# Where the low halves of streamed weights are made: by a GpSimd subtraction, or by an accumulating DMA

## The chip, the cores and the metric

The program runs on one core of a Trainium2 chip. The metric is the device time of one execution in microseconds. The kernel before takes 3158.84 us (median of three runs, 3158.76 to 3171.22).

Engines go by short names here: PE multiplies matrices (PEld loads its weights), DVE, ACT and POOL (GpSimd) do elementwise work, SP issues DMAs. Each engine works through its own list in order, and semaphores hold it where it needs another's result. Sixteen DMA engines move data between HBM and the on-chip SBUF for whoever issues a transfer.

## The reference

One decoder layer for a prompt of 2048 tokens and a sample batch of 8 x 8 tokens, width 1024. Cut to what carries work here:

```python
def hybrid_layer(x, c, r0, s0_re, s0_im, pos0, w_ada, b_ada, norm1_g, norm2_g, w_in, ...):
    mod = (jnp.einsum('bd,de->be', jax.nn.silu(c), w_ada) + b_ada).astype(x.dtype)
    sh1, sc1, gt1, sh2, sc2, gt2 = jnp.split(mod[:, None, :], 6, axis=-1)
    h = rms_norm(x, norm1_g) * (1 + sc1) + sh1
    z = jnp.einsum('bld,de->ble', h, w_in)
    q, k, v, g, u, gate_r, gate_s = jnp.split(z, IN_SPLITS, axis=-1)
    ...
    ret, r_new = retention(q, k, v.reshape(...), r0)
    ret = rms_normalize(ret).reshape(bsz, seq_len, RET_V_W) * jax.nn.silu(g)
    ssm, s_re, s_im = s5(u, s0_re, s0_im, ...)
    ssm = jax.nn.gelu(ssm)
    ssm = ssm * jax.nn.sigmoid(jnp.einsum('blc,ce->ble', ssm, w_glu))
    branch_r = jnp.einsum('blc,cd->bld', ret, w_br)
    branch_s = jnp.einsum('blc,cd->bld', ssm, w_bs)
    merged = jax.nn.sigmoid(gate_r) * branch_r + jax.nn.sigmoid(gate_s) * branch_s
    x = x + gt1 * jnp.einsum('bld,de->ble', merged, w_out)
    h2 = rms_norm(x, norm2_g) * (1 + sc2) + sh2
    ff = jnp.einsum('blf,fd->bld', jnp.square(jax.nn.relu(jnp.einsum('bld,df->blf', h2, w_up))), w_down)
    return x + gt2 * ff, r_new, s_re, s_im
```

Everything is float32. The kernel gets its precision from a rounded format that PE takes (float32r): a number x is split into a high half hi = round(x) and a low half lo = x - hi, and a product is made of three matmuls, hi·hi, hi·lo and lo·hi.

## The kernel before, in words

**Stages.** The prompt is worked through in four super-blocks of 512 tokens; then one feed-forward stage does w_up and w_down for all tokens, with a block scheme of its own that does not pass through the lines changed here. Each super-block runs the matmul blocks u, q, k, v, g, gr0, gs0, gr1, gs1 (columns of w_in), glu, br0, br1, bs0, bs1 and wo0, wo1. Beside the second super-block's prompt rows run the sample's. The first super-block has eight blocks "ada" (columns of w_ada) between its own. In the third, w_up for the sample runs as a "side" stream (us0 to us7), in the fourth w_down (ds0, ds1): after each weight unit of the main list, one unit of the side list is used.

**The weight stream.** All these weights come through one stream of 312 units of 128 x 2 x 512 float32, 512 KB each: 86 for the first super-block, 54 for the second, 86 each for the third and the fourth. `plan` fixes the order. `fetch` (L181) loads a unit from HBM into one of four raw buffers by a DMA that SP issues. `refill` (L183 on) splits it: ACT copies the raw unit to the rounded high half `whi` (L191), and one engine subtracts, `wlo` = raw - `whi` (L194): DVE for the ada units and for half of the side units, POOL for all the others. `whi` and `wlo` have five buffers each (RING). A main unit is used by 24 prompt matmuls of 128 x 512 (L253), an ada or a side unit by 4 (L259, L227). `refills` in `block` takes up a new unit after the first quarter of the next one; in the wo blocks of the first three super-blocks (order "j") four units are held until the block's last quarter.

**Order.** The kernel is written as one program; a scheduler in the framework then sets the order of the instructions on each engine, by its own model of how long things take. So an edit of a few lines can change the order in other places. Only the first five units of the stream (`keep`) stay in the order they are written in.

**What else DVE, POOL and ACT do in these stages.** DVE: norms (L606, L610: steps of a reciprocal square root on 128 x 1 values), S5 scans (L1200), evacuation of PSUM banks. POOL: `hl` at the start (L665), part of the rotary (L1531), `sl` and `ml`, low halves of activations (L1621, L1674). ACT: copies and tanh out of PSUM.

Of the kernel before, what the change touches and what calls it, by code (L numbers as in the profile page):

```python
# [13 lines left out]
AF = mybir.ActivationFunctionType  # L14
ALU = mybir.AluOpType
# [12 lines left out]
SIDE = ('us', 'ds')  # L28
# [54 lines left out]
class Layer:  # L83
# [101 lines left out]
    def refill(self, keep=False):  # L185
        nc = self.nc
        if self.split < len(self.stream):
            raw = self.rawq.pop(self.split)
            hi = self.ring.tile([P, 2, 512], F32R, name="whi")
            lo = self.ring.tile([P, 2, 512], F32R, name="wlo")  # L190
            a = nc.scalar.activation(hi, raw, AF.Copy)  # L191
            name = self.stream[self.split][0][:2]
            eng = nc.vector if name == "ad" or name in SIDE and self.split % 4 < 2 else nc.gpsimd
            l = eng.tensor_sub(lo, raw, hi)  # L194
            if keep:
                self.tc.keep_in_program_order(a)
                self.tc.keep_in_program_order(l)
            self.wq[self.split] = (hi, lo)
            self.split += 1
        self.fetch()  # L200
# [1605 lines left out]
```

## Time and profile before

| | |
|---|---|
| Median of three runs | 3158.84 us |
| The profiled execution, device time | 3166.64 us |
| Its span in the profile | 3164.8 us |
| Mean granted PE clock | 0.958 |
| Busy: PE, DVE, POOL, ACT | 2930.6, 1942.0, 1761.4, 1219.9 us |
| Moved by DMA | 516.23 MB on SP's queue, 52.1% of the 16 engines' span |

The stages lie so in the profile (by the first matmuls of their banks): setup 0 to 63 us, the four super-blocks 63 to 523, 523 to 980, 980 to 1402 and 1402 to 1814 us, feed-forward from 1814 us on. "Idle before" and "waits" are put down to what came last; L12 is line 12 of the kernel. [...] In the change, lines after L193 stand three lines lower (L253 before is L256 after).

### The profile page before, as it was taken

How to read it: one execution, taken by the hardware profiler on the slowest of the kernel's cores; microseconds unless marked ns; L12 is line 12 of the kernel's file. 1: busy time of each engine (PE TensorE's matmuls, PEld its weight loads, DVE VectorE, ACT ScalarE, POOL GpSimd, SP SyncE). 2: the span in 40 equal slices, each digit the busy share in tenths (PEclk: the TensorE clock that was granted, in tenths of full speed). 3: DMA queues.
4: the chain of work that ended last, by engine and by line, in shares of the span. 5: the costliest groups of instructions: out<-in, count | busy, mean ns of one | idle time of the engine just before them, and what ended most of it. 6: DMA issues, size and time to landing. Idle time of an engine off the chain costs nothing. (4 is left out here: it accounts for less than half of the span.)

```text
span 3164.8 us, 37143 instructions
## 1 busy us (share of the span) xinstructions
PE 2930.6 (93%) x13436; PEld 2389.0 (75%) x13436; DVE 1942.0 (61%) x3116; ACT 1219.9 (39%) x1876; POOL 1761.4 (56%) x1028
## 2 busy tenths in 40 slices
PE   7789999999989899999899799999999999997995
PEld 3568777788777688777788687787778888876884
DVE  4979674771667875667743556655556655456554
ACT  2233442122423234423234354455334555553332
POOL 2331454334344545555345486668888666588881
PEclk9889999999999899999999899999999999998998
DMA  8466435543345954458544645556444654466442
GB/s 219 154 193 215 148 103 166 158 137 107 91 108 185 254 173 126 127 173 239 164 134 132 192 156 173 180 180 207 163 146 161 205 173 154 153 226 212 141 146 80
DMA packets 336556, 518.61 MB, mean 164 GB/s; under 512 B 71270, under 2 KB 168054, under 8 KB 332267
## 3 DMA queue, kind: packets, MB, share of 16 engines
q1 hardware_dynamic: 336372, 516.23, 52.1%
q8 instruction: 106, 1.74, 0.2%
q14 instruction: 78, 0.64, 0.1%
HBM read 401.39 MB, written 114.78 MB: 163 GB/s over the span
## 5 line engine op out<-in xcount | busy, mean ns | idle before, releaser
L194 POOL TENSOR_TENSOR wlo<-wraw,whi 128x1024 fp32r<-128x1024 f32 x248 | 613.0, 2483 | 760.8 <-ACT whi L191 655.2
L399 PE MATMUL pq_down<-shi,tw 128*128 128x512 f32 x1792 | 569.4, 397 | 36.5 <-DVE acc L459 26.1
L191 ACT ACTIVATE whi<-wraw 128x1024 fp32r<-128x1024 f32 x312 | 324.0, 1056 | 652.3 <-issue 79.6
L399 PE MATMUL pq_up<-shi,tw 128*128 128x512 f32 x1792 | 560.5, 393 | 13.2 <-ACT tw L310 7.7
L399 PEld LDWEIGHTS pq_down<-shi,tw 128*128 128x128 f32 x1792 | 342.4, 191 | 115.8 <-issue 22.5
L399 PEld LDWEIGHTS pq_up<-shi,tw 128*128 128x128 f32 x1792 | 340.2, 190 | 86.4 <-ACT tw L310 8.8
L311 POOL TENSOR_TENSOR tw<-traw,tw 128x512 fp32r<-128x512 f32 x192 | 286.9, 1509 | 146.9 <-ACT tw L310 146.5
L391 DVE TENSOR_TENSOR slo<-sw,shi 128x1024 fp32r<-128x1024 f32 x140 | 233.4, 1679 | 197.2 <-ACT shi L390 164.2
L399 PE MATMUL pq_down<-slo,tw 128*128 128x512 f32 x896 | 354.1, 395 | 0.0
L399 PE MATMUL pq_up<-slo,tw 128*128 128x512 f32 x896 | 352.2, 393 | 0.8 <-DVE slo L391 0.8
L390 ACT ACTIVATE shi<-sw 128x1024 fp32r<-128x1024 f32 x140 | 147.1, 1057 | 256.1 <-DMA sw<-sd 184.5
L459 DVE SCALAR_TENSOR_TENSOR acc<-pq_down,modT,acc 128x512 f32<-128x512 f32 x224 | 159.3, 743 | 91.7 <-PE pq_down L399 91.2
L399 PEld LDWEIGHTS pq_down<-slo,tw 128*128 128x128 f32 x896 | 171.4, 191 | 35.2
L399 PEld LDWEIGHTS pq_up<-slo,tw 128*128 128x128 f32 x896 | 170.3, 190 | 36.4 <-DVE slo L391 1.1
L310 ACT ACTIVATE tw<-traw 128x512 fp32r<-128x512 f32 x224 | 136.1, 624 | 60.9 <-PE pq_down L399 51.6
L409 ACT ACTIVATE aq<-pq_up 128x512 f32<-128x512 f32 x128 | 72.4, 590 | 183.8 <-PE pq_up L399 183.8
L194 DVE TENSOR_TENSOR wlo<-wraw,whi 128x1024 fp32r<-128x1024 f32 x64 | 85.7, 1340 | 67.9 <-ACT whi L191 63.8
L345 POOL TENSOR_TENSOR ts<-traw,ts 128x512 f32<-128x512 f32 x64 | 97.2, 1518 | 51.7 <-issue 48.8
L311 POOL TENSOR_TENSOR tw<-t,tw 128x512 fp32r<-128x512 f32 x64 | 102.4, 1611 | 33.4 <-ACT tw L310 33.4
L253 PE MATMUL pd_wo<-whi,mh 128*128 128x512 f32 x256 | 102.0, 402 | 16.2 <-DVE tw L1692 16.0
L310 ACT ACTIVATE tw<-ts 128x512 fp32r<-128x512 f32 x128 | 80.2, 626 | 91.0 <-PE pq_up L399 78.6
L345 POOL TENSOR_TENSOR ts<-traw 128x512 f32<-128x512 f32 x64 | 85.6, 1338 | 51.9 <-DMA traw<-in_w_up_dram 29.6
(531 smaller groups left out, 6726.2 us busy)
## 6 DMA issues: line engine op xcount, KB each, us to landing
wraw<-in_w_in_dram SPq DMA_DIRECT2D x144, 512.0 KB
sw<-sd SPq DMA_DIRECT2D x112, 512.0 KB
s5p<-s5c SPq DMA_DIRECT2D x32, 1024.0 KB
traw<-in_w_up_dram SPq DMA_DIRECT2D x64, 512.0 KB
sd<-sq SPq DMA_DIRECT2D x32, 1024.0 KB
sd<-aq SPq DMA_DIRECT2D x32, 768.0 KB
traw<-in_w_down_dram SPq DMA_DIRECT2D x24, 1024.0 KB
wraw<-in_w_ada_dram SPq DMA_DIRECT2D x32, 512.0 KB
```

Source lines behind the costliest of these rows:

```text
L191: a = nc.scalar.activation(hi, raw, AF.Copy)
L194: l = eng.tensor_sub(lo, raw, hi)
L253: nc.tensor.matmul(banks[j], a, b, start=(k == 0 and z == 0), stop=(k == nk - 1 and z == 2))
L310: self.nc.scalar.activation(t[:, 0], x, AF.Copy)
L311: eng.tensor_sub(t[:, 1], x, t[:, 0])
L345: G.tensor_sub(x[p], l, x[m] if isinstance(m, int) else m)
L390: nc.scalar.activation(hi[:, a], t, AF.Copy)
L391: V.tensor_sub(lo[:, a], t, hi[:, a])
L399: self.nc.tensor.matmul(bank, w, x, start=(first and a == 0 and z == 0), stop=(a == 3 and z == 2), skip_group_check=True)
L409: copy = lambda d, b: nc.scalar.activation(d, b, AF.Copy)
L459: V.scalar_tensor_tensor(d, b, g, d, op0=ALU.mult, op1=ALU.add)
```

## The change

Three things are edited in `refill`. Which engine subtracts is no longer chosen by a list: the first five units (`keep`) and the ada units are subtracted by DVE. For every other unit ACT writes the negated high half into `wlo` (a copy with scale -1 from `whi`, L196), and then a DMA that POOL issues (L197) reads the unit's weights from HBM a second time and adds them onto `wlo`: lo = -hi + raw. The rest of the program is as it was.

```diff
             a = nc.scalar.activation(hi, raw, AF.Copy)
             name = self.stream[self.split][0][:2]
-            eng = nc.vector if name == "ad" or name in SIDE and self.split % 4 < 2 else nc.gpsimd
-            l = eng.tensor_sub(lo, raw, hi)
+            if keep or name == "ad":
+                l = nc.vector.tensor_sub(lo, raw, hi)
+            else:
+                nc.scalar.activation(lo, hi, AF.Copy, scale=-1.0)
+                nc.gpsimd.dma_start(lo, self.stream[self.split][1], accum_op=ALU.add)
             if keep:
                 self.tc.keep_in_program_order(a)
                 self.tc.keep_in_program_order(l)
```

In the built program POOL's 248 subtractions are gone and 276 accumulating DMAs stand on POOL; ACT has 276 more instructions (2017 in place of 1741), DVE 28 fewer tensor operations (36 subtractions of weights in place of 64). SP issues the same 1121 DMAs. The scheduler has also moved rows on every engine. Three places:

POOL, where the third super-block begins (`ml`: low halves for its neighbour wo1; `nq`, `ab`: quarters of the normed rows, L704 and L709). Before:

```order
L1674 TENSOR_TENSOR ml<-tb,mh 128x512
L194 TENSOR_TENSOR wlo<-wraw,whi 128x1024 x9
L704 TENSOR_TENSOR nq<-ab,nq 128x512
L709 TENSOR_TENSOR ab<-ab,nq 128x512
L194 TENSOR_TENSOR wlo<-wraw,whi 128x1024 x4
```

With the change:

```order
L1677 TENSOR_TENSOR ml<-tb,mh 128x512 x4
L197 DMA wlo<-in_w_out_dram 128x2x512 x4
L197 DMA wlo<-in_w_in_dram 128x2x512
L197 DMA wlo<-in_w_up_dram 128x2x512
L197 DMA wlo<-in_w_in_dram 128x2x512
L197 DMA wlo<-in_w_up_dram 128x2x512
```

The subtractions have become DMAs, and units of the main list (`w_in`) and of the side list (`w_up`), which POOL and DVE shared before, now all stand on POOL, in turn.

ACT, a little later in the third super-block, behind the copy of a sample bank `ps_us` and the evacuation `aS`. Before:

```order
L729 ACTIVATE aS<-pas 128x4x64
L191 ACTIVATE whi<-wraw 128x1024 x7
L740 ACTIVATE st<-ps_us_7815 64x512
L191 ACTIVATE whi<-wraw 128x1024
L729 ACTIVATE aS<-pas 128x4x64
```

With the change:

```order
L732 ACTIVATE aS<-pas 128x4x64
L191 ACTIVATE whi<-wraw 128x1024
L196 ACTIVATE wlo<-whi 128x1024
L191 ACTIVATE whi<-wraw 128x1024
L196 ACTIVATE wlo<-whi 128x1024
L191 ACTIVATE whi<-wraw 128x1024
```

Each high half is now followed by the negated copy, so a run of seven splits is fourteen instructions long.

PE, first super-block, where gs0 (bank `pd_gs`) begins behind an ada block; `po`, `prt` and `pkv` are retention's. Before:

```order
L253 MATMUL pd_gs_2577<-hh,whi 128x512
L1305 MATMUL po<-vU,rw 128x128
L253 MATMUL pd_gs_2577<-hl,whi 128x512
L253 MATMUL pd_gs_2574<-hh,wlo 128x512
L253 MATMUL pd_gs_2574<-hh,whi 128x512
```

With the change:

```order
L256 MATMUL pd_gs_2601<-hh,whi 128x512
L1308 MATMUL po<-vU,rw 128x128
L256 MATMUL pd_gs_2601<-hl,whi 128x512
L1310 MATMUL po<-R,qU 128x128
L1308 MATMUL po<-vU,rw 128x128
L1310 MATMUL po<-R,qU 128x128
L1308 MATMUL po<-vU,rw 128x128
L1310 MATMUL po<-R,qU 128x128
L1308 MATMUL po<-vU,rw 128x128
L1310 MATMUL po<-R,qU 128x128
L1328 MATMUL prt<-cpk,rw 128x128 x4
L1316 MATMUL pkv<-vU,rw 128x128 x4
```

In the change the first product with `wlo` comes only behind these rows of retention: the scheduler has put work between the matmuls that need only the high half and those that need the low one.

## The prediction

> **What bounds the kernel now.** I read the page's first part, then busy time by stage, then PE's waits, then the rows of the operations that the edit touches. In the first rows of windows the columns are start and end of the stretch, its length, busy time of PE, PEld, DVE, ACT, POOL, the PE clock, the busy share of the DMA engines, and GB/s.
>
> ```profile
> span 3164.8 us, 37143 instructions
> 63.00:523.00 460.00, 413.91 (x1977) 332.81 (x1978) 356.84 (x727) 159.74 (x231) 175.86 (x83) 0.93 0.53 161
> 523.00:980.00 457.00, 436.00 (x2114) 361.47 (x2113) 254.69 (x544) 126.39 (x197) 182.65 (x95) 0.96 0.43 125
> 980.00:1402.00 422.00, 391.73 (x1882) 325.42 (x1881) 291.37 (x509) 154.27 (x225) 223.65 (x104) 0.96 0.59 173
> 1402.00:1814.00 412.00, 380.94 (x1812) 318.31 (x1812) 242.67 (x413) 146.19 (x196) 201.24 (x93) 0.96 0.57 173
> ```
>
> The four super-blocks, 1751 us, are the only stage in which the weight stream runs. PE sets their length: it idles 46 + 21 + 30 + 31 = 128 us there. POOL, whose work is taken away, is busy for about 45% of them, and is no bound. Who ends PE's idle time? PE's waits, longest first (total, times, longest):
>
> ```profile
> PE pd_wo L253 <- DVE tw L1692: 16.0, 3, 10.0
> PE py L1215 <- DVE s5t L1207: 14.6, 8, 3.5
> PE pd_k L253 <- DVE rt L1530: 12.5, 3, 10.2
> PE pt L650 <- DVE xr L643: 9.4, 4, 2.7
> PE pms L735 <- DVE mS L1655: 8.9, 1, 8.9
> PE pw L1128 <- DVE s5bx L1121: 8.0, 1, 8.0
> PE pt L886 <- DVE mt L880: 7.9, 1, 7.9
> PE prt L1325 <- DVE rw L1321: 7.9, 3, 4.0
> PE pd_v L253 <- DVE rt L1530: 5.3, 3, 3.7
> ...
> PE ps_ds L227 <- DVE wlo L194: 0.8, 1, 0.8
> ...
> PE pd_wo L253 <- ACT hh L664: 0.2, 1, 0.2
> ```
>
> Nine rows that belong to the super-blocks wait for DVE: 90.5 us together. For a low half PE waited 0.8 us in the whole run, and that one came from DVE. So the subtraction on POOL is hidden completely, and taking it away gives nothing by itself. What the edit can win is DVE's time; what it can lose is DMA time and punctual low halves.
>
> **What it removes.** The operations, as minimum/median/maximum ns, and POOL's as a group (total us, mean ns, idle before):
>
> ```profile
> L194 POOL TENSOR_TENSOR wlo<-wraw,whi x248: 2339/2400/4042, 55.7 to 1781.2; 128x1024 fp32r<-128x1024 f32 x124
> L194 DVE TENSOR_TENSOR wlo<-wraw,whi x64: 1198/1220/3175, 78.1 to 1661.6; 128x1024 fp32r<-128x1024 f32 x64
> L191 ACT ACTIVATE whi<-wraw x312: 1038/1060/1079, 54.2 to 1780.1; 128x1024 fp32r<-128x1024 f32 x156
> L181 SPq DMA_DIRECT2D wraw<-in_w_in_dram x144: 362/368/3301, 36.6 to 1662.8; - x144
> ...
> L194 POOL TENSOR_TENSOR wlo<-wraw,whi 128x1024 fp32r<-128x1024 f32 x248 | 613.0, 2483 | 760.8 <-ACT whi L191 655.2 <-PE ps_ada L259 30.0 <-PE ps_wo L259 26.9
> ```
>
> 248 x 2.48 us leave POOL, 28 x 1.2 = 34 us leave DVE. There is a second effect. Three groups of small DVE operations, first as source views (minimum/median/maximum), then as groups (total, mean):
>
> ```profile
> L610 DVE SCALAR_TENSOR_TENSOR y<-t,y x162: 143/161/2395, 21.7 to 3137.5; 128x1 f32<-128x1 f32 x96, 128x4 f32<-128x4 f32 x48, 64x1 f32<-64x1 f32 x9, 128x8 f32<-128x8 f32 x6
> L606 DVE SCALAR_TENSOR_TENSOR t<-y,v x105: 195/220/2396, 21.5 to 2029.8; 128x1 f32<-128x1 f32 x96, 64x1 f32<-64x1 f32 x9
> L1200 DVE TENSOR_TENSOR_SCAN s5t<-cs,g,s5t x128: 313/326/2455, 241.8 to 1568.7; 128x64 f32<-128x64 f32 x128
> ...
> L606 DVE SCALAR_TENSOR_TENSOR t<-y,v 128x1 f32<-128x1 f32 (+1 forms) x105 | 75.3, 717 | 2.9
> L610 DVE SCALAR_TENSOR_TENSOR y<-t,y 128x1 f32<-128x1 f32 (+4 forms) x162 | 68.3, 422 | 4.7
> ```
>
> An operation on one number per partition, 0.16 us at its median, takes up to 2.40 us: the length of one POOL subtraction. DVE is held up beside POOL's work. Mean less median, times the count: 105 x 0.497 = 52 us and 162 x 0.261 = 42 us in two groups alone. These steps lie in chains (norms, S5) that PE waits for. So part of the 90.5 us can go; its bounds are 0 and 90.5. In the last two super-blocks DMA will set the pace (below) and eat it; in the first two I take 30 us, a third of the whole.
>
> **What it adds on ACT and POOL.** 276 negated copies of 1.06 us are 293 us on ACT, whose four stages rise from 587 to 880 of 1751 us: half, which is no bound. An evacuation behind a pair waits 1.06 us longer; the only row in which a matmul of these stages waits for an ACT result (above) has 0.2 us, so there is room. POOL issues 276 DMAs: at SP's price, 0.37 us, 102 us, at the price of the subtraction that each replaces 662 us, against 608 before; either way hidden. While POOL waits for ACT's negated copy, its `sl`, `ml` and rotary additions stand behind it, as they stood behind the wait for `whi` before.
>
> At the start the five kept subtractions move to DVE. Two of them now stand ahead of the bias addition of the last ada bank:
>
> ```profile
> 61.79 0.68 DVE L855 TENSOR_TENSOR mt<-ps_ada,ba 9x512 f32<-9x512 f32 x1 [6.77 <-PE ps_ada L822]
> ```
>
> DVE idles 6.8 us there, which covers 2 x 1.2 us. Without that cover it would cost 2.4 us. I take 0.
>
> **What it adds on DMA: the main term.** 276 more transfers of 512 KB, 145 MB. No row shows an accumulating DMA, so I bound its price p in time of all 16 engines. A plain move, from a stretch of 100 us in the feed-forward stage where large rows dominate:
>
> ```profile
> 2700.00:2800.00 100.00, 97.39 (x423) 80.02 (x422) 52.90 (x52) 53.23 (x79) 66.98 (x46) 0.98 0.45 158
> ```
>
> 158 GB/s at a busy share of 0.45 is 351 GB/s when busy: 524,288 bytes take 1.49 us. Lower bound: p = 1.49, if reading the old contents costs nothing. But the sum needs two inputs, the weights from HBM and the -hi that lies in SBUF; if both go through the same engine, p = 2 x 1.49 = 2.99. Upper bound: two moves, and the addition as slow as POOL's, 2.99 + 2.48 (its mean) = 5.47. I take 2.99.
>
> The Trainium skill has a rule for this, on the page "Collectives: The Full Stack", in the section on the bandwidth ceiling (fold count, why AG ≠ RS ≠ AR): a transfer that reduces is half as fast as one that copies, since it reads two sources through one queue, and not since the addition costs cycles. By that rule the sum below is the forecast; by a price of one move it is rival A. No row here shows which.
>
> By stage, busy DMA time before plus the units there (50, 54, 86, 86 accumulations) at 2.99 us:
>
> - first: 0.53 x 460 = 244, + 150 = 393 of 460 us;
> - second: 0.43 x 457 = 197, + 161 = 358 of 457 us;
> - third: 0.59 x 422 = 249, + 257 = 506 of 422 us: 84 us too much;
> - fourth: 0.57 x 412 = 235, + 257 = 492 of 412 us: 80 us too much.
>
> The last two don't fit. A look at one pair of units there, by PE's pace:
>
> ```profile
> 1063.99 0.40 PE L253 MATMUL pd_k<-hh,whi 128*128 128x512 f32 x1
> ...
> 1069.90 0.39 PE L253 MATMUL pd_k<-hh,wlo 128*128 128x512 f32 x1
> ```
>
> 26 starts in 5.91 us: 0.227 us a matmul. A main unit and a side unit take 24 + 4 matmuls, 6.4 us; their two loads and two accumulations would take 2 x 1.49 + 2 x 2.99 = 9.0 us of DMA. And where DMA is full already, PE pays today:
>
> ```profile
> 1020.00:1040.00 20.00, 19.64 (x97) 15.94 (x96) 17.33 (x36) 5.69 (x6) 12.56 (x6) 1.00 0.97 268
> 1040.00:1060.00 20.00, 10.25 (x43) 8.34 (x41) 7.91 (x12) 3.77 (x4) 8.61 (x6) 0.74 1.08 306
> ```
>
> With the DMA engines at 1.08 PE is busy for half of the stretch.
>
> **Sum.** 84 + 80 - 30 = +134 us. The profiled execution took 3166.6 us (span 3164.8), 7.8 us above the median: 3301 against it, 3293 against the median. I forecast 3290 us.
>
> **Rivals.**
>
> A, faster. The accumulation costs one move, p = 1.49. Then the third super-block has 249 + 128 = 377 of 422 us, the fourth 363 of 412: it fits, and DVE's relief comes in all four. With a third to half of 90.5 us: about -35, 3124 us. For it: POOL's hold on DVE is in the rows (2395 ns), PE's longest waits are for DVE. Against: the second source. It decides below p = 2.0, from where (422 - 249) / 86 fills the third super-block. The Trainium skill ("SBUF — State Buffer", Who interferes with whom) says that a DVE instruction with two inputs from SBUF contends with a GpSimd one that reads SBUF, not with one that only writes; by that rule issuing DMAs would leave DVE free of this, and no run here shows POOL issuing DMAs.
>
> B, a little slower: the DMA fits, but the low half comes late. Before, ACT and POOL needed 1.06 + 2.40 = 3.5 us from a free buffer to the low half. Now ACT 2 x 1.06, issue 0.37 and a transfer of 2.0 us are 4.5 us, 6.5 if another queue takes every second turn. Behind an ada block the buffer's lead is 16 ada matmuls and the 8 that need only the high half, 24 x 0.227 = 5.4 us. Eight such places at 1 to 3 us are up to 24 us; the stretch 1020 to 1060 us, full already, holds 40 x 86 / 422 = 8 units: 16 us more. +40 without relief: 3199, say 3200 us. Against: PE's order was changed to put more work ahead of the low halves.
>
> C, far slower: p = 5.47. The super-blocks exceed by 57, 35, 297 and 293 us: +682, 3841 us. Nothing in the rows speaks for so slow an addition but that none excludes it.
>
> D, no effect: it fits, and PE's waits for DVE stay, because DVE's chains are long even at their medians: 3159 us.
>
> That the edit doesn't do what it says is out: the built program has 276 accumulating DMAs and no subtraction on POOL.
>
> **How the numbers follow.** Chances: forecast 0.42, A 0.24, B 0.14, C 0.12, D 0.08. The forecast's own range is p from 2.5 to 3.5: excess 80 to 252 us, less 30: 3209 to 3381 us. Eight in ten: from 3115 (a third of A, 0.08, is left below) to 3540 (C, 0.12, is left above). A measurement of this kernel tells 0.5%, 16 us, from no change: faster 0.24 (A), same 0.08 (D), slower 0.68 (the forecast, B, C).
>
> **What would show it.** Right: a DMA share near 1 in the third and fourth super-block, which last some 505 and 490 us, with the feed-forward stage as long as before (1351 us); a queue of POOL's with about 145 MB whose packets cost twice a plain one's; PE waiting for `wlo` by DMA; L606 and L610 near their medians of 0.22 and 0.16 us. Wrong: a DMA share under 0.9 in these two, or super-blocks as long as before; L610 still at 0.42 us would refute the relief, and POOL busy or waiting for a free queue in long stretches, with `ml` and `sl` late for PE, would be a mechanism that I haven't counted.

## The result and the profile after

The changed kernel takes **3735.72 us** (median of four runs, 3726.28 to 3748.22) against 3158.80 us for the kernel before on the same chip: a ratio of **1.1805**, 95% interval 1.1773 to 1.1837. The forecast was 3290 us, in a range of 3115 to 3540. The direction was right and the size was not: 577 us were lost where 131 were expected.

First the super-blocks again, with the columns of the prediction's windows: start and end, length, busy time of PE, PEld, DVE, ACT, POOL, PE clock, DMA share, GB/s. The fifth row is the feed-forward stage.

```profile
61.50:597.40 535.90, 442.15 (x1981) 351.76 (x1980) 285.62 (x729) 208.74 (x284) 103.38 (x80) 0.89 0.76 188
597.40:1087.50 490.10, 441.56 (x2113) 360.90 (x2112) 211.90 (x543) 178.94 (x250) 116.54 (x94) 0.95 0.76 175
1087.50:1736.20 648.70, 463.22 (x1882) 368.75 (x1881) 204.71 (x494) 237.66 (x312) 144.93 (x118) 0.82 0.79 181
1736.20:2374.30 638.10, 442.84 (x1811) 349.23 (x1809) 184.66 (x397) 228.22 (x279) 132.51 (x109) 0.84 0.78 181
2374.30:3724.50 1350.20, 1265.65 (x5536) 1038.21 (x5536) 776.78 (x847) 620.14 (x1005) 968.46 (x648) 0.97 0.50 169
```

The feed-forward stage is as long as before (1351 us). All of the loss is in the four super-blocks, most of it in the third and the fourth, which grew from 422 and 412 to 649 and 638 us. But there the DMA engines are busy for 0.79 and 0.78 of the time, not for all of it: the overload on which the forecast rested isn't what sets the time, and a share under 0.9 in these two was the prediction's own first sign of being wrong. Nothing else is full either: POOL, for one, is busy for about a fifth of these stages.

PE idles for 93.8 + 48.5 + 185.5 + 195.3 = 523 us in the super-blocks (length less busy), against 128 before. These are its longest waits:

```profile
PE pd_gr L256 <- DMA wlo<-in_w_in_dram: 71.5, 17, 7.7
PE pd_wo L256 <- DMA wlo<-in_w_out_dram: 51.5, 15, 11.6
PE pd_q L256 <- DMA wlo<-in_w_in_dram: 49.7, 12, 7.5
...
PE po L1310 <- POOL R L1320: 27.9, 4, 11.4
PE pd_wo L256 <- POOL ml L1677: 26.7, 6, 13.1
```

Thirteen such rows, 417 us in 120 waits, are for a low half that a DMA brings; before there was one such wait, of 0.8 us. Two further rows, 54.6 us, wait for POOL's own products, `R` and `ml`. What is POOL late for? Its waits (total, times, longest), and the time from the start of its DMAs to their landing:

```profile
POOL wlo L197 <- issue: 834.4, 135, 13.6
POOL wlo L197 <- ACT wlo L196: 235.2, 38, 22.2
```

```profile
DMA to landing us min/median/max: 5.6/6.4/16.1
```

"issue" is a wait for which the profile has no releaser. POOL stood for 834 us ahead of its DMAs with nothing that the profile can name to wait for. POOL's timeline early in the third super-block shows the rhythm (start, duration, instruction, idle time before):

```profile
1153.58 1.22 POOL L197 DMA_DIRECT2D wlo<-in_w_in_dram  x1 [7.44 <-ACT wlo L196]
1162.08 1.21 POOL L197 DMA_DIRECT2D wlo<-in_w_up_dram  x1 [7.27 <-issue]
1168.58 1.22 POOL L197 DMA_DIRECT2D wlo<-in_w_in_dram  x1 [5.29 <-issue]
...
1174.94 1.21 POOL L197 DMA_DIRECT2D wlo<-in_w_up_dram  x1 [3.82 <-issue]
```

The DMAs start 6.4 to 8.5 us apart: about as long as one of them takes to land. Counted over the whole trace, no accumulation starts before the one ahead of it has landed, and 244 of the 275 intervals end 0.30 to 0.33 us after that landing. **POOL's accumulating DMAs run one at a time.** At the median of 6.4 + 0.3 us, 86 of them need 576 us in a super-block that lasted 422 us; the intervals' own median, with POOL's other work between, is 7.0 us, which makes 603. The program has no such wait: POOL's DMA waits for ACT's copy, and for the readers and the DMA of the buffer five units back.

Two signs that the prediction named came true. POOL's queue carries 145 MB, and its packets take 24.0% of the span on 16 engines, so one unit costs 0.24 x 3724.5 / 276 = 3.24 us: price p, taken as 2.99. And the small DVE operations became short: the means were 717 and 422 ns before.

```profile
q0 software_dynamic: 75072, 144.72, 24.0%
```

```profile
L613 DVE SCALAR_TENSOR_TENSOR y<-t,y 128x1 f32<-128x1 f32 (+4 forms) x162 | 35.8, 221 | 4.9
L609 DVE SCALAR_TENSOR_TENSOR t<-y,v 128x1 f32<-128x1 f32 (+1 forms) x105 | 32.5, 309 | 3.1
```

### The profile page after: what moved, and what is told of

Same layout as the page of the kernel before. It is cut to its first block, busy times and chain, and to the rows that moved or that the text cites. A ratio compares the mean times of both kernels' runs of the same rounds, so it can differ in the third digit from the quotient of the medians.

```text
span 3724.5 us, 37753 instructions
## 1 busy us (share of the span) xinstructions
PE 3097.0 (83%) x13436; PEld 2480.8 (67%) x13436; DVE 1688.5 (45%) x3088; ACT 1486.0 (40%) x2152; POOL 1471.1 (39%) x1056
## 5 line engine op out<-in xcount | busy, mean ns | idle before, releaser
L197 POOL DMA_DIRECT2D wlo<-in_w_in_dram x140 | 170.7, 1219 | 867.6 <-issue 376.8
L196 ACT ACTIVATE wlo<-whi 128x1024 fp32r<-128x1024 f32 x276 | 286.5, 1051 | 3.7
L256 PE MATMUL pd_gr<-hh,wlo 128*128 128x512 f32 x256 | 113.1, 455 | 71.5 <-DMA wlo<-in_w_in_dram 71.5
L256 PE MATMUL pd_wo<-wlo,mh 128*128 128x512 f32 x256 | 109.7, 429 | 51.6 <-DMA wlo<-in_w_out_dram 51.5
L256 PE MATMUL pd_gs<-hh,wlo 128*128 128x512 f32 x256 | 106.0, 426 | 40.9 <-DMA wlo<-in_w_in_dram 40.9
L256 PE MATMUL pd_wo<-whi,ml 128*128 128x512 f32 x256 | 107.2, 425 | 26.7 <-POOL ml L1677 26.7
L197 POOL DMA_DIRECT2D wlo<-in_w_out_dram x32 | 39.5, 1234 | 227.3 <-issue 91.2
```

Source lines behind the costliest of these rows:

```text
L196: nc.scalar.activation(lo, hi, AF.Copy, scale=-1.0)
L197: nc.gpsimd.dma_start(lo, self.stream[self.split][1], accum_op=ALU.add)
L256: nc.tensor.matmul(banks[j], a, b, start=(k == 0 and z == 0), stop=(k == nk - 1 and z == 2))
```

## The experiments

The theory after the result: the room that the program sets aside for the transfers that POOL issues (`dynamic_dma_scratch_size`, 1024 bytes in the last lines of the kernel) holds only one of these accumulations, so each waits for the landing of the one before. The rivals: an accumulating DMA always runs alone, whatever the room; the price p alone sets the time; or the reordering does.

### A control with one raw buffer less

The room takes SBUF, and there is none left. A raw buffer and a buffer of the feed-forward ring (`tring`) make way for it, and this run has that edit alone.

```diff
-RING, RAW = 5, 4
+RING, RAW = 5, 3
...
-        self.tring, self.traw = pool("tring", 8), pool("traw", 3)
+        self.tring, self.traw = pool("tring", 7), pool("traw", 3)
```

> Control for the next run: the change with three raw buffers in place of four and seven `tring` buffers in place of eight, which frees SBUF; the room for the descriptors of POOL's transfers stays at 1024 bytes per partition. A unit's raw buffer is given back after ACT's first copy, so nobody should miss the fourth. Both theories: within 1% of the changed kernel, 3700 to 3775 us, and POOL's transfers still start 0.3 us after the one before has landed, 6 to 7 us apart.

3722.41 us, ratio 1.1756 (1.1705 to 1.1808). In the super-blocks the buffers change little: 2329 us against 2313. The feed-forward stage is 8 us shorter with them, 1342 us; in all five runs that have this edit it lasts 1339 to 1342 us, in the seven others 1346 to 1358. The accumulations still run singly: 248 of 275 intervals end 0.30 to 0.33 us after a landing, and none ends before it.

### More room: 4096 and 2048 bytes

The same program as the control, instruction by instruction on each engine, with one number changed.

```diff
-    nc = _bacc.Bacc("TRN2", target_bir_lowering=False, num_devices=1, dynamic_dma_scratch_size=1024)
+    nc = _bacc.Bacc("TRN2", target_bir_lowering=False, num_devices=1, dynamic_dma_scratch_size=4096)
```

> The same kernel, instruction by instruction, with 4096 bytes of descriptor room in place of 1024. Theory 'one in flight' (POOL cannot issue an accumulation before the previous one has landed, because its descriptors fill the room): the starts come closer than the 5.6 us that one needs to land, POOL's idle time without a releaser (834 us) falls below 200 us, the DMA share in the third and fourth super-block rises from 0.78 to 0.9 or more, and the time falls to 3300 to 3500 us, where the DMA engines' load decides (86 x 3.24 us beside 249 and 235 us: 106 and 102 us too much, so some 3370). Theory 'load' of the prediction, with the engines' time alone: nothing changes, 3735 us. Theory 'late low half' (a fixed delay per transfer, several in flight): nothing changes either.

> The control with three raw buffers again, with 2048 bytes of descriptor room, half of the step to 4096. Theory 'room': the plain transfers of the run without the addition stood two deep in 1024 bytes, the accumulations one deep; 2048 bytes hold two accumulations, so starts can come before the landing of the one before, POOL's unexplained idle time falls from some 830 us to under 250 us, and the time lies between the two, nearer to the larger room: 3320 to 3450 us. If only a far larger room helps (a threshold between 2048 and 4096 bytes): 3700 us.

With 4096 bytes 3303.35 us, ratio 1.0433 (1.0399 to 1.0467); with 2048 bytes 3297.95 us, ratio 1.0415 (1.0382 to 1.0448), better than was expected of it. One number of the program takes away 419 of the 559 us that the control lost. The windows of the four super-blocks with 4096 bytes:

```profile
66.00:545.90 479.90, 420.15 (x1979) 338.81 (x1979) 293.67 (x729) 209.24 (x284) 102.56 (x80) 0.92 0.82 211
545.90:1023.40 477.50, 443.90 (x2114) 366.18 (x2114) 213.23 (x543) 179.08 (x250) 119.71 (x94) 0.94 0.76 179
1023.40:1492.00 468.60, 405.52 (x1882) 331.84 (x1881) 206.99 (x494) 237.71 (x312) 146.58 (x119) 0.93 1.03 252
1492.00:1964.40 472.40, 391.19 (x1811) 321.21 (x1809) 175.75 (x397) 228.35 (x279) 135.73 (x109) 0.92 0.98 244
```

POOL's longest waits and the landing times of the same run:

```profile
POOL wlo L197 <- ACT wlo L196: 833.8, 182, 34.1
```

```profile
DMA to landing us min/median/max: 5.7/10.0/18.3
```

POOL's wait without a releaser is gone; POOL now waits for ACT, as the program says. 217 of 275 accumulations start before the one ahead has landed. Each takes longer (10.0 us at the median against 6.4) and still the whole is shorter, since several share the engines. Now the third and fourth super-block have a DMA share of 1.03 and 0.98: this is the run that the prediction described. (The share can read over 1 because it adds up packets that overlap in time, those of one queue too: in the stretch from 1040 to 1060 us of the kernel before, at 1.08, all but one of 7383 packets are SP's.) That an accumulation must run alone is refuted, and so is that the price p or the order of the work alone cost the 577 us: the order is the control's, and p is still 0.246 x 3304.1 / 276 = 2.95 us.

How many of POOL's transfers are under way can be counted at each issue, the new one included. With 1024 bytes it is never more than one, with 2048 bytes up to three, with 4096 up to five, as many as `wlo` has buffers. With 2048 bytes no accumulation starts before the third one ahead of it has landed, and 41 start 0.26 to 0.40 us after that. If bytes alone limit the number, one accumulation takes more than 512 and at most 683 of them (an estimate from these counts: one and not two in 1024, three and not four in 2048).

### The old room, pieces of half the size

```diff
-                nc.gpsimd.dma_start(lo, self.stream[self.split][1], accum_op=ALU.add)
+                for h in range(2):
+                    nc.gpsimd.dma_start(lo[:, h], self.stream[self.split][1][:, h], accum_op=ALU.add)
```

> The change with each accumulation issued as two transfers of 256 KB, at the old room of 1024 bytes and with four raw buffers. Theory 'room' (bytes of descriptors, not the number of transfers, fill it): two halves are under way at once, the fixed part of the 6.4 us from start to landing is covered by the other half, and a unit takes about 5 instead of 6.3 us: 3400 to 3600 us. Theory 'one transfer at a time': each half waits for the one before, a unit takes 2 x (1.2 + 2 + 1.5) us, over 9 us: 4300 us or more.

3307.32 us, ratio 1.0445 (1.0411 to 1.0478): with 1024 bytes of room and all four raw buffers, the same work in 552 pieces of 256 KB is as quick as with four times the room. 508 of 551 pieces start before the one ahead has landed. POOL still waits without a releaser, 258 times for 276 units:

```profile
POOL wlo L198 <- issue: 426.9, 258, 7.6
```

So the room is still tight, but it holds three pieces: 444 of the 552 start with two others under way, none with three. That is enough to keep the engines supplied. The expectation of 3400 to 3600 us was a miss, in favour of the theory of room: what counts is how much of the room one transfer takes, and three pieces in 1024 bytes take at most 341 each.

### A plain DMA in place of the accumulating one

```diff
-                nc.gpsimd.dma_start(lo, self.stream[self.split][1], accum_op=ALU.add)
+                nc.gpsimd.dma_start(lo, self.stream[self.split][1])
```

> The transfer of POOL without the addition: the weights overwrite the negated half (the subtraction is left out). Theory 'one in flight': still one at a time, each start about 0.3 us behind the landing before; landing falls from 6.4 us by the 1.3 to 1.7 us that a second source costs, to some 4.8 us, so 86 x 5 = 430 us a super-block where 422 were: 3200 to 3400 us. Theory 'load': at 1.5 us a transfer of all engines everything fits (0.9 of the third super-block), 3125 to 3160 us. Price of the second source: packets of 2048 bytes at 84 ns in place of 178.

3167.54 us, ratio 1.0008 (0.9989 to 1.0026). The expectation by the theory of room was a miss: at 1024 bytes 179 of 275 plain transfers start before the one ahead has landed, and up to three are under way. The theory of load gave 3125 to 3160 us, a little too low as well. POOL needs 0.716 us to issue one, against 1.21 for an accumulating one, and the queue's time is 16.4% of the span:

```profile
L197 POOL DMA_DIRECT2D wlo<-in_w_in_dram x140: 716/716/937, 88.3 to 1680.5; - x140
```

```profile
q0 software_dynamic: 75072, 144.72, 16.4%
```

That is 0.164 x 3166.6 / 276 = 1.88 us a unit. The number of packets and the bytes are those of the accumulating run. So an accumulation takes up more of POOL's time than a copy with as many packets, and more of the room: by the counts over 512 bytes, where the copy takes at most 341. What it is that fills the room is not settled by these runs.

### The subtraction taken away, without the second reading

```diff
-                nc.gpsimd.dma_start(lo, self.stream[self.split][1], accum_op=ALU.add)
```

> The change without its transfer: `wlo` stays at the negated high half (the weights' low halves are left out of the computation). No POOL subtraction, no accumulation, ACT's negated copies remain. Relief of DVE reaches PE by a third of 90 us: 3158 - 30 = 3130 us (3110 to 3145). If PE's waits for DVE don't depend on POOL's subtractions: 3159 us within 0.5%. If ACT's 293 us more are on the path: above 3180 us.

3079.26 us, ratio 0.9717 (0.9689 to 0.9744), 84 us faster than the kernel before where 30 were forecast. The sum rows of the four super-blocks, of the kernel before and then of this run (total length; busy time of each engine; means):

```profile
sum 1750.90, PE 1622.48 PEld 1337.91 DVE 1145.60 ACT 586.60 POOL 783.20; mean PE 405.62 PEld 334.48 DVE 286.40 ACT 146.65 POOL 195.80
```

```profile
sum 1672.60, PE 1607.18 PEld 1331.03 DVE 876.67 ACT 845.63 POOL 174.45; mean PE 401.80 PEld 332.76 DVE 219.17 ACT 211.41 POOL 43.61
```

DVE's busy time falls by 269 us. Only 28 subtractions, 34 us at 1.2 us each, were taken from it. Nearly all of the other 235 us are operations that stayed: 2129 of them, the same number of each kind in both traces, take 232 us less, since they no longer last longer beside a POOL subtraction. PE's idle time falls from 128 to 65 us, and it falls where DVE was waited for: PE's waits for DVE's results go from 106 to 37 us, those for everything else from 23 to 28. Three of the prediction's longest rows, 16.0 us for `tw`, 12.5 for `rt` and 14.6 for `s5t`, read in this run:

```profile
PE pd_wo L255 <- DVE tw L1694: 7.4, 1, 7.4
...
PE pd_k L255 <- DVE rt L1532: 4.1, 2, 2.7
...
PE py L1217 <- DVE s5t L1209: 1.4, 1, 1.4
```

Three of the four super-blocks are 20 to 37 us shorter, the last two among them; the second is as long as before (423, 458, 402 and 389 us against 460, 457, 422 and 412).

### Half the bytes, with ample room

What are the 140 us that remain with 4096 bytes? Either the load of the DMA engines, or that each low half comes later. This run has the 4096 bytes and the buffers of the control, keeps all the DMAs and halves their bytes. The diff is against the run with 4096 bytes.

```diff
-                nc.gpsimd.dma_start(lo, self.stream[self.split][1], accum_op=ALU.add)
+                nc.gpsimd.dma_start(lo[:, 0], self.stream[self.split][1][:, 0], accum_op=ALU.add)
```

> The change with room for several accumulations, as in the run with 4096 bytes, but each DMA adds only the first of a unit's two rows per partition: half the bytes, the same number of DMAs. The second row of those low halves stays at the negated high half, so a part of the computation is left out. The question is what the 138 us that remain with ample room are. If they are the load of the DMA engines, the price per unit falls from 2.95 to about 1.5 us, the third super-block needs 249 + 86 x 1.5 = 378 of 422 us, and with DVE's relief the time is 3090 to 3150 us, the third and the fourth super-block back below 422 and 412 us. If they are a lateness of each low half that doesn't go by its bytes, these two stay above 440 us and the time is over 3200 us.

3139.26 us (3127.81 to 3144.85), ratio 0.9914 (0.9886 to 0.9942), as the load has it. The queue and the last two super-blocks:

```profile
q0 software_dynamic: 39744, 72.37, 14.0%
```

```profile
974.40:1390.60 416.20, 386.93 (x1881) 321.59 (x1880) 207.65 (x494) 235.83 (x311) 120.36 (x118) 0.97 0.88 229
1390.60:1794.90 404.30, 375.44 (x1811) 313.79 (x1809) 174.79 (x397) 226.01 (x280) 106.31 (x109) 0.97 0.87 232
```

One unit costs 0.14 x 3133.7 / 276 = 1.59 us; the share is 0.88, and the two stages are 5 to 8 us shorter than before. The run without a second reading and the three whose DMAs overlap make a curve. For each: the time that POOL's queue takes of 16 engines (its share times the span), the measured time, and what that is above the run without a second reading.

| Run | POOL's queue, us of 16 engines | Time, us | Above |
|---|---|---|---|
| no second reading | 0 | 3079 | 0 |
| half the bytes accumulated | 0.140 x 3133.7 = 439 | 3139 | 60 |
| all bytes, plain | 0.164 x 3166.6 = 519 | 3168 | 88 |
| all bytes accumulated, 4096 bytes of room | 0.246 x 3304.1 = 813 | 3303 | 224 |

Load costs before the engines are full on a stage's average: at a share of 0.88 already 60 us. And the fuller they are, the more each further microsecond of load costs: 60 us for the first 439, 28 for the next 80, 136 for the next 294, which is 0.14, 0.35 and 0.46 each. The runs differ in more than their load (plain or accumulating, room, buffers; the second row was taken on another chip, where the kernel before took 3166 us), but the lengths of the four super-blocks alone give the same shape: 59, 87 and 226 us above.

### All subtractions on DVE

If POOL's hold on DVE is worth 84 us, the subtractions could go to DVE itself. The kernel before, with its choice of an engine replaced:

```diff
-            eng = nc.vector if name == "ad" or name in SIDE and self.split % 4 < 2 else nc.gpsimd
-            l = eng.tensor_sub(lo, raw, hi)
+            l = nc.vector.tensor_sub(lo, raw, hi)
```

> The kernel before with all 312 subtractions on DVE: no DMA is added, no instruction on ACT, and POOL has none of them. The run without any low half took 3079 us, 84 us less than before. If that gain is DVE's freedom from POOL's subtractions (2.4 us holds on operations of 0.2 us), it remains in part, since DVE's own 248 subtractions of 1.2 us are 300 us, about what the holds cost: 3090 to 3140 us. If the gain was only less work for DVE, this is slower than before: 3170 to 3250 us.

**3121.84 us** (3117.02 to 3125.87), ratio 0.9858 (0.9834 to 0.9883): this version beats both kernels. Its sum row for the four super-blocks:

```profile
sum 1703.80, PE 1606.23 PEld 1325.47 DVE 1193.42 ACT 585.95 POOL 183.25; mean PE 401.56 PEld 331.37 DVE 298.36 ACT 146.49 POOL 45.81
```

248 subtractions at 1.22 us, 303 us, came to DVE, and its busy time rose by only 48. The other 255 us were time in which DVE's operations had been held up: the 2129 that stayed take 230 us less here too.

### Every third unit by an accumulating DMA

```diff
-            if keep or name == "ad":
+            if keep or name == "ad" or self.split % 3:
```

> Every third unit by the accumulating DMA (room 1024 bytes, as in the change), the other units, the kept and the ada ones on DVE. One accumulation in three units: about 15 us apart where one takes 6.4, so no queue; DMA load in the third super-block 249 + 29 x 3.0 = 336 of 422 us. Theory 'room': no loss by it, and 92 subtractions fewer on DVE than with all on DVE: 3085 to 3130 us. If the load or the late low half of a single accumulation costs by itself: slower than with all on DVE, 3150 to 3250 us.

> Every third unit by an accumulating DMA, the others subtracted by DVE, as in the run that took 3149 us, but with a descriptor room of 2048 bytes (three raw buffers). If that run lost its 27 us against all subtractions on DVE by single accumulations standing in POOL's queue one after the other, this one takes 3110 to 3130 us; if by the DMA engines' load or by the reordering, it stays at 3140 to 3160 us.

3149.28 us, ratio 0.9951 (0.9937 to 0.9965), with 1024 bytes of room; 3135.85 us, ratio 0.9909 (0.9880 to 0.9938), with 2048. The first was a miss: it was expected to beat the version with all subtractions on DVE, and is 27 us behind it. In its trace no accumulation starts before the one ahead has landed, though only 9 of 90 stand directly behind a landing; with 2048 bytes 11 of 90 overlap. The second lies between its two expectations, which looks as if the room explained half of the 27 us. It explains nothing of it: the four super-blocks last 1731 us with 1024 bytes and 1734 us with 2048, against 1704 with all subtractions on DVE. The 13 us between the two runs lie outside of them, 5 ahead and 12 in the feed-forward stage, which is shorter in every run with the control's buffers. So the loss of 27 to 30 us stays with either room; whether it is the load of the 91 transfers (9.1% of 16 engines in both) or the order of the work is open.

## Why the prediction was wrong

**The step that failed** is in the part on ACT and POOL: "POOL issues 276 DMAs: at SP's price, 0.37 us, 102 us, at the price of the subtraction that each replaces 662 us, against 608 before; either way hidden." It counted POOL's time to issue and took for granted, without saying so, that several transfers would be under way. An accumulation of 512 KB fills the room of 1024 bytes, so POOL's next one starts only when it has landed. Its price to the stage isn't 3 us of the DMA engines but 6.7 us of elapsed time, 576 us for 86 units against the 506 us that the forecast had for the third super-block. The control against 4096 bytes of room shows what it is worth: 3722 less 3303 = **419 us**. The number 1024 stood in the program; no row of the profile of before shows what it limits, since nothing there goes through POOL's queue. The sentence on "POOL busy or waiting for a free queue in long stretches, with `ml` and `sl` late for PE" named the sign, but gave it neither a price nor a chance, and nothing in the range up to 3540 us stood for it.

**What the sum holds without that term.** In runs of one chip, beside 3163 us for the kernel before:

| Term | Forecast | Measured | From |
|---|---|---|---|
| DVE relieved | -30 | -84 | no second reading, 3079 |
| Load of the DMA engines | +164 | +224 | room of 4096 bytes, 3303, less 3079 |
| POOL one at a time | 0 | +419 | control, 3722, less 3303 |
| Sum | +134 | +559 | |

With ample room the change costs 140 us, and 134 were forecast. That agreement is luck: both terms were too small, by 54 and by 60 us, and the errors cancel. (In the super-blocks alone it costs 148 us; the feed-forward stage is 11 us shorter with the buffers of that run.)

**Relief, under-sized.** The bounds were 0 and 90.5 us, the nine longest rows of waits for DVE (all such waits of the super-blocks are 106 us); the truth lay near the upper one, and was taken at a third. The rows would have allowed more: two groups of small operations gave 94 us of hold-up, and the whole of DVE had 235. The expectation that the last two super-blocks can't use the relief holds for this change only. The mechanism is confirmed three times, with the subtraction left out, moved to DVE, or replaced by a DMA. Of the 63 runs of L606 and L610 over 0.6 us in the trace before, 34 lie beside an L194 on POOL and the other 29 beside another POOL tensor operation; after the change 20 runs over 0.6 us are left of the same two lines, each of them beside another POOL tensor operation.

**Load, right in price, wrong in shape.** p was measured at 3.24 us in the change and 0.246 x 3304.1 / 276 = 2.95 with ample room; 2.99 was taken. The Trainium skill ("Collectives: The Full Stack", bandwidth ceiling) says of a ReduceScatter in a ring of cores that it runs at half the rate of an AllGather, since its addition reads two sources. Here the traces agree in part: 2.95 is 1.98 times the 1.49 us that the prediction took for a plain unit on SP's queue, but only 1.57 times the 1.88 us of the plain copy on POOL's own queue with as many packets. The step that compared busy time with a stage's length put the loss into the last two super-blocks alone, 84 and 80 us, and counted the first two as free. With ample room these four are 20, 20, 47 and 61 us longer than before (480, 478, 469 and 472 against 460, 457, 422 and 412). PE's waits for transfers in the first two are 43 and 25 us, where they were 0 and 5. The averages of these stages hid full stretches, as the first shows. The DMA row of the page with 4096 bytes of room, 40 slices of 82.6 us:

```profile
DMA  8796799877579999999999974655544744466442
```

The first super-block ends in the seventh slice, and it has three slices at 9 in a stage whose mean is 0.82. The curve above says the same: a load that fits on average costs time.

**Rival A** gave 3124 us for a price under 2.0 us. The plain DMA has 1.88 us and gains nothing (1.0008); half the bytes, 1.59 us, gain 0.9%, of which 12 us come from the shorter feed-forward stage. The gain of the relief is real, and the load takes it back earlier than A's threshold said.

**Rival B**, a late low half, is what PE's waits show, at ten times its size (417 us, not 40) and for another reason: not the path of one unit, which takes 2 x 1.05 + 6.4 us, but the queue of units ahead of it. With ample room the landing takes 10.0 us at the median, longer than in the change, and PE waits for low halves for 83 us in all; with half the bytes 19 us. **C** had nearly the right time (3841 us) by a price that no run shows. **D** is refuted by the run without the second reading.

**Right as forecast:** ACT's copies (276 of 1.05 us) don't set the pace (PE's waits for ACT in the super-blocks are 15 us after and 9 before); the feed-forward stage kept its length; the start kept its length (the first super-block begins at 61.5 us, before at 63), though four subtractions came to DVE there and not five: one of the kept units was DVE's before.

## What to carry to other kernels

Before work is given to transfers, ask how many of them can be under way at once on the queue that issues them: a transfer that waits for the landing of the one ahead costs its whole latency (here 6.7 us), not its share of the bandwidth (3.2 us). Where POOL issues large accumulating DMAs, make the pieces small enough that several fit into the room set aside, or enlarge the room; a wait on POOL with no releaser in front of a DMA is the sign. And an engine that is only 45% busy can still cost a neighbour: taking the subtractions from POOL and giving them to DVE, which had more work of its own, was worth 1.4%.

## What was not expected of the hardware

- **One number of the program, 419 us.** 1024 bytes of room hold one accumulation of 512 KB, 2048 bytes hold three and are as good as 4096 (3298 and 3303 us), and 1024 hold three pieces of 256 KB (3307 us) or three plain copies of 512 KB.
- **An accumulating DMA costs POOL more too:** 1.21 us to issue, against 0.72 us for a plain one with as many packets.
- **Issuing DMAs didn't hold DVE up.** The 20 long operations after the change all lie beside a tensor operation of POOL's, none beside an issue alone. It isn't for want of chances: 26 of these operations ran beside an issue alone, and the longest took 0.23 us. The Trainium skill ("SBUF — State Buffer", Who interferes with whom) says that a GpSimd instruction that only writes SBUF doesn't contend with a two-input DVE one. If an issue is such an instruction, which no run here shows, the trace agrees.
- **PE became slower where it waited.** In the third super-block its matmuls took 463 us after and 392 before, at a granted clock of 0.82 against 0.96. Of the 562 us by which the super-blocks grew (sum row below, 1790 us busy against 1622), 395 are idle time and 167 are longer matmuls. With ample room the clock is back at 0.92 to 0.94. Which of the two, waits or clock, brings the other about was not tried.

```profile
sum 2312.80, PE 1789.76 PEld 1430.64 DVE 886.90 ACT 853.55 POOL 497.37; mean PE 447.44 PEld 357.66 DVE 221.72 ACT 213.39 POOL 124.34
```
